# The third chunk's first head projections, written ahead of the last head's recurrence of the first two chunks

## The chip, the cores and the metric

One core of a Trainium2 chip runs the kernel. Its five engines each work off a queue of their own: TensorE (PE, with its weight loads as PEld), VectorE (DVE), ScalarE (ACT), GpSimd (POOL) and SyncE (SP), which here only issues transfers. The metric is the device time of one execution in microseconds; the figure for a kernel is the median of its runs.

## The reference, cut to what matters

One decoder layer over 1024 tokens of width 1024, all in 32-bit floats:

```python
h = _rmsnorm(x, norm_mix_w) * (1 + sc1) + sh1
q, f_logit, i, g, u = split(h @ w_in)          # four heads of 128, then S5's u
o_hg = _hgrn2(q, f_logit, i, g, lb)            # a gated linear recurrence over time, per head
o_s5 = _s5(u, ...)                             # a diagonal state space model, gelu, a gated unit
x = x + gt1 * (concat([o_hg, o_s5]) @ w_out)
h2 = _rmsnorm(x, norm_ffn_w) * (1 + sc2) + sh2
x = x + gt2 * _peer(h2, ...)                   # product keys, top 16 of 16384 experts, 8 heads
return _rmsnorm(x, final_norm_w)
```

For a head, `_hgrn2` makes a forget gate f, a key 1 - f, a query and a value from the projections, runs a state of 128 by 128 through time, normalizes each output row by its root mean square, and multiplies by a gate made of g.

## The kernel before, in words

The tokens are worked in four chunks of 256 (numbers 0 to 3). Activations stand transposed, features on the partitions, so every projection is a row of eight accumulating matmuls of a 128 by 128 weight tile with 256 columns; a 32-bit matmul shows as two records in the trace. `proj2` makes a pair of such products into one bank named `mm`, with weights that SP loads into four buffers named `w2`.

The program text begins with the conditioning and the norms, and then a loop of eight turns (line 1314), each with the scan of one batch of four S5 groups (`s5_scan`), the tables for the batch two turns on (`s5_tables`) and one piece of the heads of chunks 0 and 1, which are worked together (`head_pieces(0, True)`, line 1238). A piece is either `hgrn_in` of a head (line 669: four `proj2`, their sigmoids, the logarithm and running sum of f, and four transposes of the value at line 705) or `hgrn_out` of a head (line 710: the recurrence). By turns 0 to 7 the pieces are in 0, in 1, out 0, in 2, out 1, in 3, out 2, out 3. In turn 6 the norm of chunk 2 is written ahead of the piece.

`hgrn_out` has eight levels (line 742 is the matmul of seven of them, line 752 that of the eighth). Each level's operands come from DVE and an exponential on ACT, and its scores are copied by a mask into one tile `sc` that all heads share. Then follow the transposes at 765, the state update, the products with state and scores (781 and 782), the squares on ACT (787), their sum and the reciprocal root on DVE (789 to 246), the scaling (792) and transposes of the result (795), which go with the gate into a tile `mixr`.

Behind the loop stand `row_consts` (eight small transposes at line 1200, which copy a gate into a row and store it), the load of the keys, and then a list of steps in `ORDER` (line 60), worked by `step` (line 1277). In it `h2` is the next piece of chunk 2, whose pieces take two heads at once: in 0, in 2, out 0, out 2. `g0` is the gelu and gated unit of S5 for chunk 0, `o0` the output projection of chunk 0, which needs all four heads of chunk 0; `N0` is its second norm, `r0` and `s0` its scores, `p0` its choice of experts. After the list come the other stages: experts of 384 tokens by gathered rows, and those of 640 tokens by dense products.

The order on an engine is made before the launch. A planner simulates the program, and on every engine it lets the instruction that is earliest in the program text go first among those that its simulation finds ready. Each engine then works its queue strictly in that order, waiting where an operand is not there. Buffers of one name are given out in turn; the names here are `mm`, `tr` and `hg` (two banks each) and the working tiles of the heads (`f`, `k`, `b`, `q`, `gg`, `v`, `sf`, `xx`, `z`, mostly two).

Of the kernel before, what the change touches and what calls it, by code (L numbers as in the profile page):

```python
# [43 lines left out]
NGB = G // GB  # L44
# [12 lines left out]
PF = 0.2  # L57
PRB = 3
N2B = 6
ORDER = "h2 g0 o0 N0 r0 s0 s0 s0 s0 p0 h2 n3 g1 h2 h2 h3 o1 h3 N1 r1 s1 h3 s1 p1 g2 h3 X o2 Y g3 N2 s1 s1 o3 N3 R2 s2 s2 p2 s2 s2 s2 p3 s2 s2 s2 Z"  # L60
SLAB = 8
NROW = 5
NH = {}
# [26 lines left out]
def hymba_kernel(  # L90
# [96 lines left out]
    def ada(n0, n1, pool=None):  # L187
        for n in range(n0, n1):
            at = T(pool, [P, D], F32, "ada", bufs=10) if pool else T(gp, [P, D], F32, "row", bufs=NROW)
            nc.sync.dma_start(at, ada_t[n])  # L190
            nc.vector.tensor_tensor_reduce(
                out=at, in0=at, in1=cond["B"], scale=1.0, scalar=0.0, op0=ALU.mult, op1=ALU.add,
                accum_out=mod[:, n : n + 1],
            )
        TT(mod[:, n0:n1], mod[:, n0:n1], adab[:, n0:n1], ALU.add)
# [4 lines left out]
    def load_x(c, rows=False):  # L200
        t0, nt = CHUNKS[c]
        if rows:
            xt = [T(gp, [P, D], F32, "row", bufs=NROW) for _ in range(NBC)]
        else:
            xt = [T(tp, [P, D], F32, "xh", bufs=NBC) for _ in range(NBC)]
        for i, xi in enumerate(xt):
            nc.sync.dma_start(xi, x[t0 + i * P : t0 + (i + 1) * P, :])
        return xt
# [67 lines left out]
    def norm_T(xt, scol, bcol, t0=None, diags=None, ks=range(0, KD, 2)):  # L276

        diags = diags or diags_of(xt)
        ng = 0 if t0 is None else min(max(T0D - t0, 0), TC)
        res = []  # L280
        for k in ks:
            pt = T(ps, [P, 2, TC], F32, "tr", bufs=2)
            hf32 = pair(tp, F32, "hT", 8)
            for i in range(2):
                for tb in range(NBC):
                    nc.tensor.matmul(
                        pt[:, i, tb * P : (tb + 1) * P], xt[tb][:, (k + i) * P : (k + i + 1) * P], diags[tb], start=True, stop=True
                    )
                ACT(hf32[:, i], pt[:, i], AF.Identity, scale=scol[:, k + i : k + i + 1], bias=bcol[:, k + i : k + i + 1])
            res += both(hf32)  # L290
            if ng:

                pn = T(ps, [P, ng // P, 2, P], F32, "tr", bufs=2)
                for i in range(2):
                    for tb in range(ng // P):
                        nc.tensor.transpose(pn[:, tb, i, :], hf32[:, i, tb * P : (tb + 1) * P], ident)
                nn = pair(tp).rearrange("p a t -> p (a t)")[:, : 2 * ng].rearrange("p (b d) -> p b d", b=ng // P)
                nc.scalar.copy(nn, pn.rearrange("p b i d -> p b (i d)"))
                nc.scalar.dma_start(h2d[t0 : t0 + ng, k * P : (k + 2) * P].rearrange("(b p) d -> p b d", p=P), nn)
            if t0 is not None and ng < TC:  # L300

                nc.sync.dma_start(
                    h2s[k : k + 2, :, t0 + ng - T0D : t0 + TC - T0D].rearrange("k p t -> p k t"), hf32[:, :, ng:]
                )
        return res
# [286 lines left out]
    def s5_out(c):  # L592
        mixT = [None] * 4
        c0 = CHUNKS[c][0] // CT
        V3 = lambda t: t.rearrange("p (s c) -> p s c", s=CT)
        yts, ysp = [], []
        for m in range(0, 4, 2):
            yt = pair(tb_["p"], F32, "yt", 2)
            for i in range(2):
                nc.scalar.dma_start(  # L600
                    V3(yt[:, i]), ys[:, 4 * (m + i) : 4 * (m + i) + 4, :, c0 : c0 + TC // CT].rearrange("s h g c -> (h g) s c")
                )
            ACT(yt, yt, AF.Gelu)
            yts.append(yt)
            ysp += both(yt)
        for m in range(0, 4, 2):
            pt = proj2(w_glu, m, ysp, 4)
            sgm = pair(tp)
            for i in range(2):
                ACT(sgm[:, i], pt[:, i], AF.Sigmoid, bias=glub[:, m + i : m + i + 1])  # L610
            mx = pair(tb_["p"], F32, "mix", 2)
            for i in range(2):
                TT(mx[:, i].rearrange("p (c s) -> p s c", s=CT), V3(yts[m // 2][:, i]), V3(sgm[:, i]), ALU.mult)
            mixT[m : m + 2] = both(mx)
        return mixT
# [189 lines left out]
    def out_proj(c, mixT, xt):  # L805
        t0 = CHUNKS[c][0]
        for m in range(0, KD, 2):
            pt = proj2(w_out, m, mixT)
            mt = pair(tp)
            for i in range(2):  # L810
                ACT(mt[:, i], pt[:, i], AF.Copy, scale=mod[:, 16 + m + i : 17 + m + i])
            pn = T(ps, [P, NBC, 2, P], F32, "tr", bufs=2)
            for i in range(2):
                for tb in range(NBC):
                    nc.tensor.transpose(pn[:, tb, i, :], mt[:, i, tb * P : (tb + 1) * P], ident)
            for tb in range(NBC):
                xs = xt[tb][:, m * P : (m + 2) * P]
                TT(xs, xs, pn[:, tb].rearrange("p i d -> p (i d)"), ALU.add)
        for tb in range(NBC):
            r = t0 + tb * P  # L820
            nc.sync.dma_start(x1d[r : r + P, :], xt[tb])
# [416 lines left out]
    def head_pieces(c, two=False):  # L1238

        t = {}  # L1240
        outs = []
        far = T(gp, [P, 2, 2, TC], F32, "acc") if c == 2 else None

        def last(h):
            outs.append(hgrn_out(hp, c == NCK - 1, h, t.pop(h), two, None if far is None else far[:, h // 2]))
            if not two:
                raws.setdefault(c, []).append((outs[-1][:, 0], outs[-1][:, 1]))

        for h in range(0, HEADS, 1 if two else 2):
            if len(t) == 2:  # L1250
                last(min(t))
                yield
            t[h] = hgrn_in(hp, h, hTs[c], hTs[c + 1] if two else None)
            yield
        for h in sorted(t):
            last(h)
            yield
        if two:
            for i in range(2):
                raws[c + i] = [(outs[h][:, i], outs[h + 1][:, i]) for h in range(0, HEADS, 2)]  # L1260
# [16 lines left out]
    def step(what, c):  # L1277

        nonlocal rp
        if what == "n":  # L1280
            hTs[c] = norm_T(*pre[c][:1], s1c, mod[:, 0:8], None, pre[c][1])
            heads[c] = head_pieces(c)
        elif what == "h":
            next(heads[c])
        elif what == "g":
            mixes[c] = s5_out(c)
        elif what == "o":
            xts[c] = load_x(c, c == NCK - 1)
            hg = [r for two in raws[c] for r in two]
            out_proj(c, hg + mixes[c], xts[c])  # L1290
        elif what == "N":
            h2Ts[c] = norm_T(xts[c], s2c, mod[:, 24:32], CHUNKS[c][0])
        elif what in "rR":
            routes[c] = score(c, h2Ts[c], h2Ts[c + 1] if what == "R" else None)
            next(routes[c])
        elif what == "s":
            next(routes[c])
        elif what == "p":
            choose(rp, c)
        elif what == "X":  # L1300
            next(heads[NCK - 1], None)
            hpx.close()
        elif what == "Y":
            rpx.close()
            rp = tb_["r"] = rp2x.enter_context(tc.tile_pool(name="rp2", bufs=1, side="right"))
        elif what == "Z":
            tbx.close()

    hgrn_consts(hp)
    with tc.tile_pool(name="sp", bufs=1) as sp:  # L1310
        prm = s5_setup(sp)
        tabs = [s5_tables(sp, b, prm, "hg") for b in range(2)]
        pieces = head_pieces(0, True)
        for b in range(NGB):
            s5_scan(sp, b, tabs[b])
            if b + 2 < NGB:
                tabs.append(s5_tables(sp, b + 2, prm, "tr"))
            if b == N2B:
                step("n", 2)
            next(pieces, None)  # L1320
            if b < 4:
                ada(16 + 8 * b, 24 + 8 * b)
            if b == PRB:
                for c in (2, 3):
                    pre[c] = load_x(c, True)
                    pre[c] = pre[c], diags_of(pre[c])
        for _ in pieces:
            pass
# [6 lines left out]
    rp2x = ExitStack()  # L1335
    for w in ORDER.split():
        step(w[0], int(w[1:] or 0))
# [111 lines left out]
```

## Time and profile before

| what | value |
|---|---|
| median of 3 runs | 2981.1 us (2968.72 to 2986.83) |
| profiled execution | 2974.75 us, its span 2973.0 us |
| PE busy | 2782.4 us (94%) |
| PEld busy | 2492.3 us (84%) |
| DVE busy | 2464.2 us (83%) |
| ACT busy | 1093.4 us (37%) |
| mean granted TensorE clock | 0.976 |

Times inside the execution count from the start of its span. The loop of eight turns ends, and the list begins, at about 400 us; the dense stage starts near 1000 us. Busy time of PE counts overlapping records once. "Idle before" of a row is the time that its engine did nothing just ahead of it, with what ended the wait.

### The profile page before, as it was taken

The numbers are of one execution on the slowest core, as the hardware profiler recorded it, in microseconds if no ns is written. First come the engines' busy times: TensorE is split into PE (matmuls) and PEld (weight loads), VectorE is DVE, ScalarE is ACT, GpSimd is POOL, SyncE is SP. The second block draws the span as 40 slices with busy tenths as digits, with TensorE's granted clock in tenths as the row PEclk, the third lists the DMA queues.
The fourth block names the chain that finished last, engine by engine and source line by source line (L and its number), as shares of the span: only waits on it lengthen the run. The fifth ranks groups of instructions, "written<-read, shape, count | busy, mean of one in ns | idle before, by whom it ended". The sixth has DMA issues, their size and how long they took to land.

```text
span 2973.0 us, 46130 instructions
## 1 busy us (share of the span) xinstructions
PE 2782.4 (94%) x16071; PEld 2492.3 (84%) x16071; DVE 2464.2 (83%) x5598; ACT 1093.4 (37%) x2405; POOL 1143.7 (38%) x1043
## 2 busy tenths in 40 slices
PE   6899989989989799999999999999999999999995
PEld 5777978778878799989998888888888888888874
DVE  7869745977799999998568888978888888888988
ACT  3224431423310688979423322222222222222222
POOL 1765100231222002333344554545555556445552
PEclk9899989999999999999999999999999999999997
DMA  9822334686766358999999999989999899999986
GB/s 335 267 82 68 109 117 160 223 286 194 250 226 191 120 195 306 349 337 358 363 340 364 327 312 330 334 310 342 348 343 335 299 337 319 322 324 321 319 302 226
DMA packets 376265, 816.69 MB, mean 275 GB/s; under 512 B 60128, under 2 KB 153952, under 8 KB 370912
## 3 DMA queue, kind: packets, MB, share of 16 engines
q0 software_dynamic: 110592, 402.70, 38.4%
q1 hardware_dynamic: 227248, 388.74, 37.7%
q10 hardware_dynamic: 38192, 22.31, 2.7%
q8 instruction: 126, 2.06, 0.3%
q14 instruction: 107, 0.88, 0.1%
HBM read 732.27 MB, written 81.36 MB: 274 GB/s over the span
## 4 chain that ended last, share of the span: by engine, by line
PE 33%; DVE 19%; issue 19%; DMA 15%; POOL 10%; ACT 4%; POOLq 0%; ACTq 0%; DVEq 0%; SPq 0%
PE mm L1087 10%; PE mm L326 10%; POOL row L957 8%; DMA row<-in_v_rows_dram,ei 7%; PE hg L1163 3%; PE s L1163 3%; PE tr L1163 2%; DVE row L982 2%; DVE acc L998 2%; DMA row<-in_u_rows_dram,ei 2%; ACT oL L1047 2%; DMA vraw<-in_v_rows_dram 2%; DMA S<-sd 1%; DVE v L256 1%; PE hg L742 1%
## 5 line engine op out<-in xcount | busy, mean ns | idle before, releaser
L1087 PE MATMUL mm<-h2T,w 128*128 128x320 f32 x6144 | 943.5, 312 | 37.0 <-ACT S L1089 26.2
L1087 PEld LDWEIGHTS mm<-h2T,w 128*128 128x128 f32 x6144 | 913.9, 189 | 47.6 <-ACT S L1089 31.3
L957 POOL DMA_INDIRECT row<-in_u_rows_dram,ei x384 | 455.5, 1186 | 1148.9 <-DVE dots L982 648.1
L957 POOL DMA_INDIRECT row<-in_v_rows_dram,ei x384 | 523.2, 1363 | 486.5 <-DVE acc L998 400.4
L326 PE MATMUL mm<-hT,w 128*128 128x256 f32 x2304 | 529.4, 384 | 3.8 <-ACT tmp L610 2.6
L998 DVE SCALAR_TENSOR_TENSOR acc<-row,dots,acc 128x1024 f32<-128x1024 f32 x381 | 487.7, 1280 | 44.6 <-DMA row<-in_v_rows_dram,ei 41.3
L326 PEld LDWEIGHTS mm<-hT,w 128*128 128x128 f32 x2304 | 434.1, 193 | 61.5 <-ACT tmp L610 3.0
L982 DVE CUSTOM_DVE_ANT_0 row<-row,h2n 128x1024 f32<-128x1024 f32 x384 | 462.2, 1216 | 26.5 <-DMA row<-in_u_rows_dram,ei 25.7
L1163 PE MATMUL hg<-v,W 128*128 128x512 f32 x1296 | 352.5, 394 | 13.9 <-DVE v L256 5.5
L1163 PE MATMUL s<-v,W 128*128 128x512 f32 x1296 | 347.4, 391 | 2.2 <-DVE dacc L1176 1.1
L255 ACT CAST v<-vraw 128x512 fp32r<-128x512 f32 x256 | 158.5, 620 | 514.1 <-DMA vraw<-in_v_rows_dram 268.2
L1163 PE MATMUL tr<-v,W 128*128 128x512 f32 x1248 | 338.2, 392 | 8.4 <-DVE dacc L1176 4.2
L1163 PEld LDWEIGHTS hg<-v,W 128*128 128x128 f32 x1296 | 244.4, 190 | 69.5 <-DVE v L256 8.7
L1163 PEld LDWEIGHTS s<-v,W 128*128 128x128 f32 x1296 | 242.6, 188 | 55.4 <-DVE dacc L1176 2.8
L1163 PEld LDWEIGHTS tr<-v,W 128*128 128x128 f32 x1248 | 234.5, 189 | 59.7 <-DVE dacc L1176 5.5
L256 DVE TENSOR_TENSOR v<-vraw,v 128x512 fp32r<-128x512 f32 x256 | 175.4, 686 | 88.9 <-ACT v L255 87.0
L256 DVE TENSOR_TENSOR w<-raw,w 128x512 fp32r<-128x512 f32 x256 | 175.3, 686 | 70.5 <-ACT w L255 64.5
L255 ACT CAST w<-raw 128x512 fp32r<-128x512 f32 x256 | 158.2, 621 | 172.8 <-PE mm L1087 159.1
L1047 ACT ACTIVATE oL<-oA,self 128x128 f16<-128x128 f16 x640 | 196.3, 414 | 4.6 <-DVE self L1033 3.9
L1089 ACT ACTIVATE S<-mm 128x320 f32<-128x320 f32 x256 | 109.3, 439 | 206.3 <-PE mm L1087 165.2
L255 ACT CAST W<-S 128x640 fp32r<-128x640 f32 x128 | 93.1, 729 | 216.9 <-PE s L1163 65.1
L1106 DVE TENSOR_TENSOR S<-S,gt 128x640 f32<-128x640 f32 x128 | 104.1, 818 | 39.8 <-DMA S<-sd 37.6
(375 smaller groups left out, 3140.1 us busy)
## 6 DMA issues: line engine op xcount, KB each, us to landing
raw<-in_u_t_dram SPq DMA_DIRECT2D x256, 256.0 KB
vraw<-in_v_rows_dram SPq DMA_DIRECT2D x256, 256.0 KB
gd<-Gs SPq DMA_DIRECT2D x40, 1024.0 KB
gt<-gd SPq DMA_DIRECT2D x32, 1280.0 KB
w<-in_w_in_dram SPq DMA_DIRECT2D x56, 512.0 KB
w<-in_w_q_dram SPq DMA_DIRECT2D x48, 512.0 KB
sd<-S SPq DMA_DIRECT2D x64, 320.0 KB
S<-sd SPq DMA_DIRECT2D x64, 320.0 KB
```

Of the source, the lines that this page charges most:

```text
L255: nc.scalar.copy(hi, src)
L256: return nc.vector.tensor_tensor(lo, src, hi.bitcast(F32), ALU.subtract)
L326: ins = nc.tensor.matmul(out, w[:, k * P : (k + 1) * P], rhs[k], start=(k == 0), stop=(k == nk - 1))
L742: nc.tensor.matmul(pt[:, c * half : (c + 1) * half].rearrange("p (n l) -> p n l", l=lsz), blk(lh, c), two(blk(xx, c))[:, :, 1, :], start=T ...
L957: g = nc.gpsimd.indirect_dma_start(out=t, out_offset=None, in_=table, in_offset=bass.IndirectOffsetOnAxis(ap=idx, axis=0))
L982: nc.vector.tensor_tensor_reduce(out=ut, in0=ut, in1=h2, scale=1.0, scalar=0.0, op0=ALU.mult, op1=ALU.add, accum_out=dots[:, j : j + 1],)
L998: STT(acc, vt, w[:, j : j + 1], acc, ALU.mult, ALU.add)
L1047: nc.scalar.mul(Al[:, i], at(A, i), sL[:, t8 + i : t8 + i + 1])
L1087: nc.tensor.matmul(pt, wk[:, i, kc], h2T[k][:, j, cs_], start=(n == 0), stop=(n == 3 * KD - 1))
L1089: ACT(g[:, cs_], pt, AF.Gelu)
L1106: TT(gv, gv, gtile[0][:, :, e % IG, :], ALU.mult)
L1163: nc.tensor.matmul(pv[tb], ws[e][:, a, tb * P : (tb + 1) * P], v2[:, b, :], start=(e == s and n == 0), stop=(e == s + SLAB - 1 and n == 2),)
```

## The change

The first `h2` of the list, the projections of heads 0 and 1 of chunk 2, is taken from the list and written into the last turn of the loop, ahead of that turn's piece (the recurrence of head 3 of chunks 0 and 1). The same instructions are issued. In the program text they now stand ahead of that recurrence, of `row_consts` and of the load of the keys; before they stood behind all three.

```diff
-ORDER = "h2 g0 o0 N0 r0 s0 s0 s0 s0 p0 h2 n3 g1 ...
+ORDER = "g0 o0 N0 r0 s0 s0 s0 s0 p0 h2 n3 g1 ...
...
             if b == N2B:
                 step("n", 2)
+            if b == NGB - 1:
+                step("h", 2)
             next(pieces, None)
```

## Rows read from the trace of the kernel before

**Rows 1.** The page: span, then each engine's busy time, share and instructions.

```profile
span 2973.0 us, 46130 instructions
...
PE 2782.4 (94%) x16071; PEld 2492.3 (84%) x16071; DVE 2464.2 (83%) x5598; ACT 1093.4 (37%) x2405; POOL 1143.7 (38%) x1043
```

**Rows 2.** Windows: length, each engine's busy time (instructions), clock, DMA share, GB/s.

```profile
360.00:380.00 20.00, 20.00 (x123) 18.41 (x122) 10.79 (x27) 10.90 (x17) 0.00 (x0) 1.00 0.36 117
380.00:400.00 20.00, 10.34 (x56) 9.25 (x56) 11.33 (x37) 9.86 (x14) 0.00 (x0) 0.75 0.25 56
```

**Rows 3.** Timeline of PE, third head: start, length, line, operation, count [idle before].

```profile
314.89 1.00 PE L742 MATMUL hg<-xx,k 128*128 128x64 f32 x8
...
320.42 1.03 PE L326 MATMUL mm<-hT,w 128*128 128x256 f32 x4
...
340.22 0.39 PE L781 MATMUL hg<-st,xx 128*128 128x128 f32 x2
```

**Rows 4.** Timeline of PE, last head's recurrence and the hole behind it.

```profile
356.31 1.00 PE L742 MATMUL hg<-xx,k 128*128 128x64 f32 x8
357.16 4.96 PE L326 MATMUL mm<-hT,w 128*128 128x256 f32 x22
...
363.69 4.54 PE L326 MATMUL mm<-hT,w 128*128 128x256 f32 x20
...
369.79 4.54 PE L326 MATMUL mm<-yt,w 128*128 128x256 f32 x20
...
375.89 0.61 PE L765 MATMUL tr<-ident,z 128*128 128x128 f32 x4
...
382.37 1.53 PE L326 MATMUL mm<-mixr,w 128*128 128x256 f32 x6 [0.20 <-DMA w<-in_w_out_dram]
383.74 0.38 PE L781 MATMUL hg<-st,xx 128*128 128x128 f32 x2
...
385.30 0.39 PE L782 MATMUL hg<-v,sc 128*128 128x128 f32 x2
395.16 1.11 PE L795 MATMUL tr<-ident,xx 128*128 128x128 f32 x4 [9.47 <-DVE xx L792]
...
396.49 1.80 PE L742 MATMUL hg<-xx,k 128*128 128x64 f32 x8
```

**Rows 5.** Timeline of ACT: a table load, the late Gelus, the squares.

```profile
342.60 1.28 ACT L676 ACT_TABLE_LOAD   x1
343.89 0.60 ACT L676 ACTIVATE sf<-mm 128x512 f32<-128x512 f32 x1
...
358.37 1.28 ACT L603 ACT_TABLE_LOAD   x1 [5.00 <-DMA yt<-ys]
...
384.69 1.28 ACT L603 ACT_TABLE_LOAD   x1 [4.54 <-DMA yt<-ys]
...
390.41 0.58 ACT L787 ACTIVATE z<-hg 128x512 f32<-128x512 f32 x1
```

**Rows 6.** Timeline of DVE: the first level's operand; the sum of squares.

```profile
352.34 0.42 DVE L727 TENSOR_TENSOR xx<-f,q 128x256 f32<-128x256 f32 x1
...
391.02 0.69 DVE L789 TENSOR_REDUCE ms<-z 128x4 f32<-128x512 f32 x1 [5.96 <-ACT z L787]
```

**Rows 7.** Timeline of PE: the last of the eight row transposes, the value's.

```profile
413.46 0.38 PE L1200 MATMUL tr<-ident,diag 128*128 128x128 f32 x2
...
417.13 0.60 PE L705 MATMUL tr<-ident,sf 128*128 128x128 f32 x4
```

**Rows 8.** Timeline of SP's queue: the keys, the last weights of the projections.

```profile
349.64 0.33 SPq L1333 DMA_DIRECT2D keyst<-in_keys_dram  x1
351.32 0.33 SPq L321 DMA_DIRECT2D w<-in_w_in_dram  x1
```

**Rows 9.** Windows of the later stages, columns as in rows 2.

```profile
440.00:560.00 120.00, 115.47 (x603) 102.02 (x603) 79.67 (x482) 31.52 (x50) 3.27 (x3) 1.00 0.46 146
560.00:1000.00 440.00, 404.34 (x2113) 358.22 (x2112) 373.25 (x1472) 107.09 (x178) 102.01 (x98) 0.95 0.69 229
```

More of the change, by code (lines that the diff above doesn't have):

```diff
@@ L59 @@
 N2B = 6
-ORDER = "h2 g0 o0 N0 r0 s0 s0 s0 s0 p0 h2 n3 g1 h2 h2 h3 o1 h3 N1 r1 s1 h3 s1 p1 g2 h3 X o2 Y g3 N2 s1 s1 o3 N3 R2 s2 s2 p2 s2 s2 s2 p3 s2 s2 s2 Z"
+ORDER = "g0 o0 N0 r0 s0 s0 s0 s0 p0 h2 n3 g1 h2 h2 h3 o1 h3 N1 r1 s1 h3 s1 p1 g2 h3 X o2 Y g3 N2 s1 s1 o3 N3 R2 s2 s2 p2 s2 s2 s2 p3 s2 s2 s2 Z"
 SLAB = 8
```

## The prediction

> **What bounds the kernel now.** I read the page first: matmuls are busy 94% of the span, weight loads 84%, VectorE (DVE) 83% [rows 1]. No engine has slack over the whole, so time is won or lost where TensorE (PE) stands still. The windows of twenty microseconds around the change come next: PE is never idle from 360 to 380, and from 380 to 400 it is busy 10.34 us of 20 at a mean granted clock of 0.75 [rows 2]. That is the only large hole in the stretch that the change touches.
>
> The timeline of PE tells what is in it. The head projections that the change moves (the rows mm<-hT) begin at 320.42 as a filler below the third head's recurrence and the last S5 scan [rows 3]. The last head's recurrence has its first level on PE at 356.31; by then 86 of the 128 projection records are done. The other 42 follow in two bursts, of 22 and 20 records, between its levels; then come the records of the gated unit of S5 (32, yt, in two rows) and the first 12 of the output projection (mixr, rows of 2, 4 and 6), and at 385.69 the recurrence's last product is out [rows 4]. There PE stops for 9.47 us: the output projection has multiplied the three heads that exist and waits for the fourth, whose final transposes (L795) start at 395.16 [rows 4]. I call that instant the gate.
>
> The timeline of ACT tells why the hole is so long. The square of the recurrence's output (L787) could go at 385.69 but starts at 390.41: ahead of it in ACT's queue stands a Gelu of the second chunk, which sat 4.54 us until its load of ys landed [rows 5]. The squares, their sum, the reciprocal root and the scaling then take from 390.41 to the gate, 4.75 us [rows 4 to 6]. So 4.7 us of the hole is a queue accident and 4.8 us is the tail's own latency.
>
> **What the change does.** It adds and removes no instruction. In the written order 64 matmuls of 8 weight tiles (128 records), four ACT passes, their table loads, some seven DVE operations, four transposes (L705) and 8 weight loads on SP go from behind the last recurrence and the eight gate-row transposes (L1200) to ahead of them. The planner gives the earlier instruction first call on an engine. What was ahead already stays: 86 of 128 records, and the sigmoids, f, k and the scan that feed them.
>
> **Step 1, the 42 records.** They no longer yield to the recurrence. 22 records run from 357.16 to 361.96 or so: 4.96 us as merged, 20 take 4.54 [rows 4], thus near 0.22 us each, and 42 cost 9.2 us. The first level, whose operand DVE starts at 352.34 [rows 6], waits for PE until 356.31 + 9.2 = 365.5. Bounds: 0, if the planner finds a hole for the level between two projections, and +9.2.
>
> **Step 2, the recurrence without those bursts.** It took 27.4 us from its first level to its first product with the state (356.31 to 383.74) [rows 4]. The third head's took 25.3 us (314.89 to 340.22) [rows 3]. I take the shorter, because only 44 filler records (9.7 us) are left to stand in its way. The first product falls at 390.8, the last at 390.8 + 1.95 = 392.8. Bounds: PE has the same records to run up to there, and it ran them gapless to 385.69, so 385.7 is the earliest; 385.7 + 9.2 = 394.9 is the latest.
>
> **Step 3, the tail.** The load that the late Gelu waits for can go once the first chunk's gated unit has freed a buffer, and that unit's records follow the same projections on PE in either order [rows 4]; so I leave ACT free at about 390.4, as before. At 392.8 nothing is left of the 4.7 us. The gate comes at 392.8 + 4.75 = 397.6, that is 2.4 us later than 395.16. So the change loses about 7 us ahead of the accident and gets 4.7 of them back from it.
>
> **Step 4, the transposes L705.** The two banks named tr are given out in program order: L705 stands at 417.13, right behind the last of L1200, although its input was ready long before [rows 7]. Moved ahead of the recurrence's own tr tiles it runs in the recurrence's shadow, and 0.4 us of PE leaves the dense output projection. It takes a bank ahead of L765. That transposition ran at 375.89 and the last projection would end near 365.5, ten microseconds earlier, so nobody waits for it.
>
> **Step 5, SP and POOL.** The last of the 8 weight loads was issued at 351.32, behind the keys at 349.64 [rows 8], and used after 363: twelve microseconds of cover. The keys load is needed only when the scores begin, after the output projection; the store of the gate row comes after L1200. POOL has nothing in this stretch. Cost 0. If that cover were gone, PE would wait for one load.
>
> **Step 6, table loads of ACT.** Gathering the projections' Sigmoid and Ln ahead of the recurrence's Exp can save a table load or add one. A load takes 1.28 us, and the next ACTIVATE starts 1.29 us after it [rows 5]; ACT is busy 10.9 us of 20 there [rows 2]. I count 0, with 1.3 us either way inside the bounds above. The Trainium skill (ScalarE: Activation LUTs, What ACT_TABLE_LOAD costs) adds a drain of about 1380 ns to each load of 1283 ns; the load's length agrees, the drain is not seen between these two rows, and by the page one more switch would be worth an estimated 2.7 us.
>
> **The clock.** After the hole the same eight matmuls of a level take 1.80 us where they took 1.00 [rows 4], the lower of two levels (1.2 and 2.4 GHz). Of the work up to 400 that can have cost at most half of 4.8 us, 2.4. A closed hole gives it back; a longer one can cost as much again. I count 0.
>
> **Sum.** +2.4 - 0.4 = +2.0 us on the profiled execution's 2974.75 us (span 2973.0) [rows 1], thus 2976.8. That execution lies 6.35 us under the median of 2981.1, so the forecast is **2983 us**. About 1% (30 us) is what a measurement of this kernel can tell from no change.
>
> **Rivals.**
>
> *The gate moves by the whole 9.2 us.* The Gelu accident moves along with it, or the recurrence needs its 27.4 us again. For it: DVE's part is a chain that no PE filler sets. Against it: the 4.54 us are ended by a landing [rows 5]. With the clock's 2.4: +11.6, **2993 us**. It decides from the point when the recurrence's last product comes after 393.
>
> *The hole closes.* The planner interleaves so that the last product stays at 385.7 and places the Gelu behind the square: -4.7 - 2.4 - 0.4 = -7.5, **2974 us**. For it: PE had its records gapless before. Against it: work that is not urgent goes ahead of work that is.
>
> *Nothing happens.* The planner ran two thirds of the projections ahead of the recurrence anyhow [rows 3, 4], and the rest may come out in the same order: **2981 us**.
>
> *The whole later plan shifts, to the worse.* The list order after 440 is made anew from shifted instants, and accidents like the Gelu fall elsewhere. PE idles 4.5 us of 440 to 560 and 35.7 of 560 to 1000 [rows 9]; where heads, scores and the first gathers share that stretch, a second 35.7 us would give **3019 us**. It decides if a third chunk's recurrence comes late against its output projection. The same *to the better* would have to take away three quarters of those 40 us: 2951 or less.
>
> **Numbers.** The forecast 0.45; whole delay 0.18; hole closed 0.12; nothing 0.15; a worse later plan 0.06; a better one 0.04. Within 1% are the first four: 0.90; slower 0.06; faster 0.04. The range takes in 2974 and 2993 and, on either side, the spread of the runs of before (2968.7 to 2986.8, 12.4 under the median and 5.7 over) with a few microseconds of a shifted later plan: 2960 to 3005. It leaves out the two ends of the later plan.
>
> **What would show it.** Right: L705 ahead of L765; one row of some 40 projection records before the first L742 of the last head, which stands near 365; L795 between 395 and 400; the Gelu's wait over before L787 is ready. Wrong, step 1: the first level still near 356 with projections behind it. Step 2: a recurrence longer than 27.4 us or well under 25. Step 3: L787 again held by a landing. The whole argument is wrong if the windows from 440 to 1000 hold a difference larger than that of 300 to 440.

## The result and the profile after

The changed kernel takes 3000.04 us (median of 6 runs, 2996.69 to 3007.00), the kernel before, measured beside it, 2979.45: a ratio of 1.0076, 95% interval 1.0058 to 1.0094. That is some 0.8% slower: inside the range, 17 us above the forecast of 2983, and by the prediction's bound of 1% still no change. But the interval is clear of 1, so the change does slow the kernel, by ten times the 2 us that the prediction summed up.

The page after answers to [rows 1]. The same 16071 records keep PE busy 14.1 us longer; the span grew by 25.2, so 11.1 us are new idle time and the rest is slower records. These are two single executions: that of before lies 4.7 us under its median, and the medians are 20.6 us apart. The 29 instructions that the page counts more are semaphore operations, which the new order brings: e3 below, with the old text, has 46159 too. Their number does not make the time, for e8 has only 46126 and is slower still.

```profile
span 2998.2 us, 46159 instructions
...
PE 2796.5 (93%) x16071; PEld 2508.3 (84%) x16071; DVE 2464.4 (82%) x5598; ACT 1093.5 (36%) x2405; POOL 1122.4 (37%) x1043
```

The windows of after, columns as in [rows 2], the stretches of [rows 2, 9] first:

```profile
360.00:380.00 20.00, 20.00 (x112) 18.04 (x111) 10.09 (x27) 10.80 (x15) 0.00 (x0) 1.00 0.48 134
380.00:400.00 20.00, 12.62 (x84) 11.53 (x84) 13.50 (x40) 11.12 (x16) 0.00 (x0) 0.92 0.28 59
440.00:560.00 120.00, 116.58 (x587) 103.13 (x588) 78.69 (x481) 28.79 (x46) 0.12 (x1) 0.95 0.45 141
560.00:1000.00 440.00, 407.97 (x2135) 361.47 (x2133) 369.15 (x1465) 106.66 (x175) 103.28 (x101) 0.95 0.69 230
1000.00:1600.00 600.00, 565.56 (x4490) 551.50 (x4490) 512.32 (x1240) 423.94 (x1266) 172.78 (x144) 0.97 0.83 302
...
2940.00:3020.00 80.00, 29.23 (x116) 23.34 (x116) 48.19 (x90) 14.44 (x32) 14.59 (x12) 0.81 0.45 156
```

The last two stretches in the kernel before:

```profile
1000.00:1600.00 600.00, 575.82 (x4591) 561.47 (x4590) 516.79 (x1240) 426.39 (x1270) 177.95 (x148) 0.99 0.86 310
...
2940.00:3020.00 80.00, 5.56 (x25) 4.28 (x23) 26.89 (x62) 7.82 (x17) 5.21 (x5) 0.84 0.20 72
```

Where the change was made nothing is lost: 380 to 400 has 9.7 us of idle PE before and 7.4 after, at a better clock. The dense stage is another matter. From 1000 to 1600 PE is idle 34.4 us where it was idle 24.2, with 101 records fewer done, and at 2940 the changed kernel has 116 records left where before had 25. Lined up by the same instruction, after stands 6.8 us behind before at the first upward product (L1087, near 994), 15.5 at the first downward one (L1163, 1577), 23.5 near 1966 and 29.1 near 2868. The first of these says little: e4 below, which has the queues of after, reaches that product at 996.8, and e1 and e2, which have before's order up to it from 520 us on, at 995.0 and 998.8.

The timeline of PE, answering to [rows 3, 4, 7]:

```profile
317.77 1.00 PE L742 MATMUL hg<-xx,k 128*128 128x64 f32 x8
...
359.19 9.23 PE L326 MATMUL mm<-hT,w 128*128 128x256 f32 x42
368.26 1.00 PE L742 MATMUL hg<-xx,k 128*128 128x64 f32 x8
...
372.21 0.60 PE L705 MATMUL tr<-ident,sf 128*128 128x128 f32 x4
...
384.97 0.60 PE L765 MATMUL tr<-ident,z 128*128 128x128 f32 x4
...
389.70 0.39 PE L781 MATMUL hg<-st,xx 128*128 128x128 f32 x2
...
391.52 0.39 PE L782 MATMUL hg<-v,sc 128*128 128x128 f32 x2
396.77 1.12 PE L795 MATMUL tr<-ident,xx 128*128 128x128 f32 x4 [4.86 <-DVE xx L792]
```

At the third head's first level this execution is 2.88 us behind that of before (317.77 against 314.89), though PE's queue up to there is the same; so 2.88 is taken off each time here. The first level of the last head then comes at 365.4 and the gate (L795) at 393.9: 1.3 us *earlier* than the 395.16 of before, with a hole of 4.86 us where there were 9.47. The runs below bear it out: from the third head's first level to the gate it is 79.0 to 79.9 us in the three kernels with the whole change (after, e2, e4) and 80.0 to 81.1 in before, e11 and the six pinned kernels with the old text.

The timeline of ACT, answering to [rows 5]:

```profile
386.26 1.28 ACT L603 ACT_TABLE_LOAD   x1 [1.88 <-DVE xx L738]
387.55 0.63 ACT L603 ACTIVATE yt<-yt 128x512 f32<-128x512 f32 x1
...
391.44 0.63 ACT L756 ACTIVATE e<-b 128x512 f32<-128x512 f32 x1 [0.95 <-DVE sth L778]
392.01 0.60 ACT L787 ACTIVATE z<-hg 128x512 f32<-128x512 f32 x1
```

The late Gelu no longer waits for its landing, and the square follows the last product at once.

So where are the 25 us? One wait of PE in the dense stage (1600 to 2940) stands out: total, times, longest. First after, then before:

```profile
PE mm L1087 <- ACT S L1089: 29.7, 10, 4.3
```

```profile
PE mm L1087 <- ACT S L1089: 13.6, 8, 2.6
```

This wait grew by 16.1 us, but PE's whole idle time there only from 36.6 to 42.2, as other waits got shorter. The windows, after and then before:

```profile
1600.00:2300.00 700.00, 685.89 (x3586) 606.59 (x3586) 590.36 (x830) 197.18 (x350) 345.46 (x271) 1.00 0.95 329
2300.00:2940.00 640.00, 611.95 (x3089) 534.95 (x3088) 543.09 (x632) 159.34 (x282) 321.88 (x242) 0.98 0.90 316
```

```profile
1600.00:2300.00 700.00, 690.99 (x3618) 610.89 (x3617) 598.14 (x837) 195.94 (x349) 358.73 (x274) 1.00 0.95 333
2300.00:2940.00 640.00, 612.41 (x3046) 528.33 (x3045) 544.77 (x636) 161.24 (x287) 331.57 (x241) 0.98 0.90 315
```

So the wait marks the mechanism and is not the whole sum. In e1 and e3 below, which differ in nothing but the later order, the same idle time goes from 32.6 to 48.7.

An upward product (24 records) needs one of two banks `mm`, and a bank comes free when ACT has taken half a gate out of it by a Gelu (L1089). One such wait, in the timelines of ACT and PE after:

```profile
2371.23 0.61 ACT L255 CAST v<-vraw 128x512 fp32r<-128x512 f32 x1
2384.08 0.62 ACT L255 CAST v<-vraw 128x512 fp32r<-128x512 f32 x1 [12.24 <-DMA vraw<-in_v_rows_dram]
2384.60 0.43 ACT L1089 ACTIVATE S<-mm 128x320 f32<-128x320 f32 x1
```

```profile
2371.52 1.18 PE L1087 MATMUL mm<-h2T,w 128*128 128x320 f32 x7
...
2374.84 6.17 PE L1087 MATMUL mm<-h2T,w 128*128 128x320 f32 x41
2385.09 6.04 PE L1087 MATMUL mm<-h2T,w 128*128 128x320 f32 x24 [4.08 <-ACT S L1089]
```

The same place before, again ACT and then PE:

```profile
2348.56 0.61 ACT L255 CAST v<-vraw 128x512 fp32r<-128x512 f32 x1
2354.86 0.44 ACT L1089 ACTIVATE S<-mm 128x320 f32<-128x320 f32 x1 [5.69 <-PE mm L1087]
2362.55 0.62 ACT L255 CAST v<-vraw 128x512 fp32r<-128x512 f32 x1 [7.25 <-DMA vraw<-in_v_rows_dram]
```

```profile
2352.03 9.84 PE L1087 MATMUL mm<-h2T,w 128*128 128x320 f32 x66
...
2364.70 12.35 PE L1087 MATMUL mm<-h2T,w 128*128 128x320 f32 x72 [2.60 <-ACT S L1089]
```

Before, ACT's queue holds the Gelu first and then the cast of a v that is still on its way; the Gelu goes as soon as its product is out, and PE gets a third product done ahead of its stop. After, the two stand the other way round. The product is complete near 2377.4 (7 records, and 17 more at 0.15 us from 2374.84), but its Gelu sits until 2384.60 behind a cast that waited 12.24 us for its landing; PE fills the second bank and stops after 48 records. It is the accident of [rows 5], a ready Gelu behind an instruction with a late load, made many times. The Trainium skill (PSUM — Partial Sum Buffer, Engine vs sequencer instructions) calls ACT's queue strictly first in, first out; these rows agree, the ready Gelu not having passed the cast. In all 9 waits of this kind over 0.5 us after, the instruction just ahead of the Gelu on ACT is a cast of v that itself stood 7 to 12 us; before, in 3 of 8. In the other 5 of before such a cast, with 5 to 7 us of standing, is three places ahead of the Gelu, as at 2362.55 above: before's order shortens the accident and does not remove it.

The changed text touches none of these instructions. But the order of every queue is made from the whole program, and it came out anew: side by side, the lists of the queues from about 520 us on (those of e1 and e3 below) hold another instruction in 4340 of 12437 places on PE, 2214 of 3496 on DVE, 1116 of 2102 on ACT, 191 of 841 on SP and none of 768 on POOL. On PE, DVE and ACT over nine tenths of these lie behind 1000.

### The profile page after: what moved, and what is told of

It is laid out like the page before. It is cut to its first block, busy times and chain, and to the rows that moved or that the text cites. A ratio compares the mean times of both kernels' runs of the same rounds, so it can differ in the third digit from the quotient of the medians.

```text
span 2998.2 us, 46159 instructions
## 1 busy us (share of the span) xinstructions
PE 2796.5 (93%) x16071; PEld 2508.3 (84%) x16071; DVE 2464.4 (82%) x5598; ACT 1093.5 (36%) x2405; POOL 1122.4 (37%) x1043
## 4 chain that ended last, share of the span: by engine, by line
PE 47%; DVE 15%; DMA 14%; issue 13%; POOL 7%; ACT 3%; ACTq 0%; DVEq 0%; POOLq 0%; SPq 0%
PE mm L1087 16%; PE mm L326 14%; POOL row L957 5%; DMA vraw<-in_v_rows_dram 4%; PE hg L1163 4%; PE s L1163 4%; DMA row<-in_v_rows_dram,ei 3%; PE tr L1163 3%; DMA row<-in_u_rows_dram,ei 3%; DVE row L982 2%; DVE acc L998 2%; ACT oL L1047 1%; DMA S<-sd 1%; PE s L1051 1%; PE s L1052 1%
## 5 line engine op out<-in xcount | busy, mean ns | idle before, releaser
L1087 PE MATMUL mm<-h2T,w 128*128 128x320 f32 x6144 | 955.1, 315 | 51.3 <-ACT S L1089 42.0
L1087 PEld LDWEIGHTS mm<-h2T,w 128*128 128x128 f32 x6144 | 924.2, 191 | 62.2 <-ACT S L1089 46.9
L957 POOL DMA_INDIRECT row<-in_v_rows_dram,ei x384 | 503.6, 1312 | 518.5 <-DVE acc L998 417.1
L1163 PE MATMUL hg<-v,W 128*128 128x512 f32 x1296 | 352.2, 394 | 15.8 <-DVE v L256 7.2
L1163 PE MATMUL s<-v,W 128*128 128x512 f32 x1296 | 346.8, 391 | 1.6 <-DVE v L256 1.5
L1163 PE MATMUL tr<-v,W 128*128 128x512 f32 x1248 | 336.8, 391 | 4.5 <-DVE v L256 2.4
L1163 PEld LDWEIGHTS hg<-v,W 128*128 128x128 f32 x1296 | 244.0, 190 | 70.2 <-DVE v L256 10.3
L1163 PEld LDWEIGHTS s<-v,W 128*128 128x128 f32 x1296 | 243.4, 189 | 53.3 <-DVE v L256 2.3
L1163 PEld LDWEIGHTS tr<-v,W 128*128 128x128 f32 x1248 | 234.0, 188 | 54.3 <-DVE v L256 3.7
L1089 ACT ACTIVATE S<-mm 128x320 f32<-128x320 f32 x256 | 109.7, 441 | 204.6 <-PE mm L1087 182.1
```

Source lines behind the costliest of these rows:

```text
L957: g = nc.gpsimd.indirect_dma_start(out=t, out_offset=None, in_=table, in_offset=bass.IndirectOffsetOnAxis(ap=idx, axis=0))
L1087: nc.tensor.matmul(pt, wk[:, i, kc], h2T[k][:, j, cs_], start=(n == 0), stop=(n == 3 * KD - 1))
L1089: ACT(g[:, cs_], pt, AF.Gelu)
L1163: nc.tensor.matmul(pv[tb], ws[e][:, a, tb * P : (tb + 1) * P], v2[:, b, :], start=(e == s and n == 0), stop=(e == s + SLAB - 1 and n == 2),)
```

## The experiments

Theory A: the loss is the re-made order of the later queues. Theory B: it is the moved projections themselves (their place, and what it does to the work after them). Eight kernels fix each queue's order from about 520 us on, by an edge from each instruction to the next one on its engine that demands order and no wait (shortened):

```diff
     ...
+    pin(nc, tc)
+def pin(nc, tc):
+    ...
+        for x, y in zip(queue, queue[1:]):
+            tc.add_manual_dep(ins[y], ins[x].name, NoSync, reason="pin")
```

Everything that is computed stays. "Wait" in this table is that of PE's L1087 for ACT's S, from 1600 to 2940, in us. The medians of before beside them are 2978.21 (e1 to e4), 2977.79 (e5 to e8) and 2979.97 (e9 to e12). The ratio is not the quotient of the medians; the two differ by up to 0.0016 (e6).

| kernel | text and order up to 520 us | order behind | median, us | ratio to before | wait |
|---|---|---|---|---|---|
| e1 | before | before | 2976.85 | 1.0003 (0.9990 to 1.0016) | 11.7 |
| e2 | changed | before | 2979.04 | 1.0008 (0.9992 to 1.0024) | 13.2 |
| e3 | before | changed | 2999.52 | 1.0080 (1.0060 to 1.0100) | 32.9 |
| e4 | changed | changed | 3000.94 | 1.0086 (1.0065 to 1.0107) | 26.9 |
| e5 | before | changed from 520 to 1370 only | 2986.70 | 1.0023 (1.0006 to 1.0040) | 17.4 |
| e6 | before | changed from 1370 on | 3005.07 | 1.0076 (1.0046 to 1.0106) | 29.4 |
| e9 | before | changed from 1370 to 1585 only | 2984.45 | 1.0015 (0.9997 to 1.0034) | 12.3 |
| e10 | before | changed from 1585 on | 2995.43 | 1.0044 (1.0023 to 1.0065) | 29.3 |
| e7 | projections behind `o0` | its own | 3004.57 | 1.0080 (1.0049 to 1.0112) | 27.1 |
| e8 | projections behind `g0` | its own | 3014.20 | 1.0114 (1.0086 to 1.0142) | 28.4 |
| e11 | projections behind the last recurrence | its own, the same as before's | 2980.53 | 1.0009 (0.9993 to 1.0026) | 11.4 |
| e12 | projections in turn 6 | its own | 3017.84 | 1.0124 (1.0091 to 1.0157) | 31.4 |

**e1 to e4, text against later order.** The edit is the function above, with one or the other list of the later order.

> The kernel before, with the order of every engine's queue from about 520 us on written down and pinned to what the planner itself made of the kernel before (no instruction differs; edges of issue order only). All theories: the same as before, 2979 us, ratio 1.000 within 0.3%. If it is not, pinning itself costs time and the other three runs are read against this one.

> The changed kernel (projections ahead of the last recurrence, so the local order up to 430 us is that of the change), with every queue from 520 us on pinned to the order of the kernel before. Theory A, the planner's later order costs the time: about 2978 to 2982 us, ratio 0.999 to 1.002, since in the two traces the gate at L795 lies 1.3 us earlier against the step before it. Theory B, the moved projections themselves cost it, in a way that the gate doesn't show: about 3000 us, ratio 1.007.

> The kernel before, with its own text and its own order up to 430 us, and every queue from 520 us on pinned to the order that the planner made of the changed kernel. Theory A: about 3000 us, ratio 1.006 to 1.009. Theory B: about 2979 us, ratio 1.000. If it lies between, both parts matter.

> The changed kernel with its own later order pinned. All theories: as the changed kernel, about 3000 us, ratio 1.007.

e1 and e4 show that the pins cost nothing that these runs can tell: both give the kernel that they copy. e2 has the whole change up to 520 us and is no slower than before; e3 has nothing of the change but the later order, and has the whole loss. The wait goes with the order. In e2, and then in e3:

```profile
PE mm L1087 <- ACT S L1089: 13.2, 8, 3.5
```

```profile
PE mm L1087 <- ACT S L1089: 32.9, 10, 5.7
```

Theory B has fallen: the moved projections are worth 1.0008, with an interval that takes in 1.

**e5, e6, e9, e10, which part of the later order.** The text is that of before, and a part of the list is exchanged, cut where both orders have issued the same instructions.

> The kernel before, pinned as in the runs above, with the order of the changed kernel only from 520 us to about 1370 us (scores, choice of experts, most of the gate maps and of the early upward products) and its own order behind that. Theory A1, the later order loses in several places and the losses add: in the traces the pinned later order had lost some 7 us against the other by then, so about 2985 us, ratio 1.002 to 1.003. Theory A2, only the dense stage loses, and what is late before it is made up: ratio 1.000.

> The kernel before, pinned, with its own order to about 1370 us and the order of the changed kernel behind it (the last early products and the dense stage). Theory A1: the other 12 to 15 us, about 2992 us, ratio 1.004 to 1.006. Theory A2: all of it, about 3000 us, ratio 1.007 to 1.009.

> The text of before with every queue pinned from about 520 us on: before's order, but from about 1370 to about 1585 us (the last early products of the dense stage, up to the first products with v) the order of the changed kernel, and behind that before's order again. Theory A (the loss is made of many small waits, wherever the re-made order lies): lining up e6 with e1 by the dense products gives 7 to 12 us by the end of this stretch, so a ratio of 1.0025 to 1.004, 2985 to 2990 us. Rival A2 (the loss is all in the reordered dense turns behind): 1.000, 2978 us. Rival A3 (a late first v sets everything back once, and the rest only follows): 1.007, 2999 us.

> The text of before with every queue pinned: before's order up to about 1585 us, the order of the changed kernel behind (the dense turns). Theory A: e6 against e1 lost some 29 of its 41 us of dense stage behind 1583 us, less what e6 spreads: a ratio of 1.004 to 1.007, 2990 to 2999 us, with waits of PE for ACT's S of 2 to 5 us at the places where e6 has them. Rival A2 (all of it here): 1.0076, 3001 us. Rival A3 (a late first v sets everything back): 1.000, 2978 us.

The three pieces e5, e9 and e10 add to 0.82%, the loss of e3. Over half of it (0.44%) is behind 1585 us, where ACT's list differs from before's in 108 places, each by at most five, as the Gelu and the cast above; e10 has the long wait there, e9 has not:

```profile
PE mm L1087 <- ACT S L1089: 29.3, 9, 5.9
```

```profile
PE mm L1087 <- ACT S L1089: 12.3, 8, 4.4
```

So the loss does not sit in one place. The new order ahead of 1370 us (e5) and that behind 1585 (e10) each cost time, with intervals clear of 1; e9's takes in 1 as well as the value that theory A expected. The late first v (A3) falls, for e9's interval ends at 1.0034 and A3 said 1.007. That the dense turns alone make it (A2) falls by e5; e10 speaks against it more weakly, its interval ending at 1.0065, below A2's 1.0076 but not below the lower end of e3's. e6 came out larger than theory A1 expected, at the value of its A2; its interval reaches both.

What makes e5's 0.23% was not separated: one wait of L1051 for the gates (Gs, L1054) ahead of 1600 is 3.8 us in e5 and 1.6 in e1, and in the dense stage, where e5 has before's order, the wait for S is 17.4 where e1 has 11.7. Nor did any run exchange the order of one engine alone. In e10 the list of DVE differs in 1352 places and that of PE in 1223, so it is shown that the order costs the time, while that ACT's casts are what costs it there is argued from the waits.

**e7, e8, e11, e12, other places for the same projections.** Nothing is pinned, and the planner makes each order. In e7 and e8 the step stays in the list and only goes later:

```diff
-ORDER = "h2 g0 o0 N0 r0 ...
+ORDER = "g0 o0 h2 N0 r0 ...      (e7)
+ORDER = "g0 h2 o0 N0 r0 ...      (e8)
```

> Nothing pinned. The moved projections go the other way: behind the output projection of chunk 0 in the list of steps, later than in the kernel before, so no recurrence waits for them. In the planned queues the order of ACT and of SP in the later stages comes out as that of the changed kernel, and that of PE and DVE nearly so. Theory A (the later order costs): about 3000 us, ratio 1.005 to 1.010, though nothing was moved ahead. Theory B (the projections ahead of the recurrence cost): 2979 us or less, ratio 1.000 or below.

> Nothing pinned. The projections stand behind the gated unit of chunk 0, one step later than in the kernel before. The planner makes a third later order of it, unlike both. Theory A: the time is that of its later order, anywhere from 0.5% faster to 1% slower, and not tied to the move. Theory B: as the kernel before, ratio 1.000.

In e11 and e12 it is taken from the list as in the change and written elsewhere in the loop:

```diff
             next(pieces, None)
+            if b == NGB - 1:
+                step("h", 2)          # e11
...
             if b == N2B:
                 step("n", 2)
+                step("h", 2)          # e12
```

> Nothing pinned. The step h2 is taken from the list and written into the last turn as in the change, but behind that turn's recurrence instead of ahead of it, so it only passes the row transposes and the keys' load. The order that it gives behind 520 us is that of before, instruction by instruction. Theory A (the time follows the later order): ratio 1.000, 2978 us, the same within 0.2%. Rival B (writing the projections earlier costs by itself): between 1.000 and 1.008, about 1.004.

> Nothing pinned. The step h2 is written one piece earlier still, in turn 6, right behind the norm of chunk 2, ahead of the recurrences of heads 2 and 3. Its later order is a fourth one, different from before's in some 4500 places of PE's queue. Theory A (a re-made later order is worth some tenths of a per cent either way and is not told by how far the projections move): 0.996 to 1.012, with the difference behind 520 us. Rival B (the time grows with how early the projections stand): above the change's 1.008, with the difference ahead of 520 us.

e11 moves the projections past the row transposes and the keys' load but not past the recurrence; the later order comes out as before's (its trace has the same instructions in the same places on PE, DVE and ACT behind 1000 us) and so does the time. e7 moves them the other way, later, and loses as much as the change does, with an order that behind 1000 us is the changed kernel's on the same three engines. e8, also later but with an order of its own, lost 1.14%, a little more than the 1% that its expectation allowed, though its interval reaches that. So the loss doesn't follow how early the projections stand. e12 is the one with a loss of its own at the place of the edit: PE waits for a Gelu and the gate comes 12.5 us later than the 395.16 of before.

```profile
373.42 2.08 PE L326 MATMUL mm<-yt,w 128*128 128x256 f32 x4 [6.38 <-ACT yt L603]
...
407.61 1.12 PE L795 MATMUL tr<-ident,xx 128*128 128x128 f32 x4 [4.85 <-DVE xx L792]
```

Its expectation, all of the difference behind 520 us, missed that; but of 43.3 us of span some 31 still come later, with the same wait (31.4 us). Every new order that the planner made is slower than before's, by 0.8 to 1.2% (e12's own loss near 400 us included), and no version beat before. That before's order is a lucky one among many fits this, but four orders don't show it.

## Why the prediction came out as it did

The forecast was "no change beyond 1%", and its local argument held up; the loss came from a place that its sum had priced at nothing. That the time still lies inside the range is luck: the range was widened for the spread of the runs and "a few microseconds of a shifted later plan", and the later plan cost some 20.

- **Step 1 was right.** 42 records in one row, first level at 365.4 against 365.5.
- **Step 2 was mis-sized.** From first level to first product with the state the recurrence took 21.4 us (368.26 to 389.70), not 25.3: the third head's run, taken as a measure, had 112 records of other work between its products (314.89 to 340.22), the last head's after only 48. That these slowed it is argued. The last product is out at 389.0, not 392.8. The prediction had named a recurrence "well under 25" as the sign against this step.
- **Step 3 was right in kind.** The Gelu's accident was absorbed and the tail took 4.86 us (4.75 expected); with step 2's size the gate comes 1.3 us earlier, not 2.4 later. The sign of the local effect was wrong by less than a run can tell: e2 gives 1.0008.
- **Step 4 was right.** L705 runs at 372.21, ahead of L765 at 384.97, and neither waits.
- **Step 5 was right.** PE runs without a gap from 358.76 to 368.26, so no weight was late.
- **Step 6 was right.** Both kernels make 74 table loads. The load at 386.26 takes 1.28 us and its ACTIVATE starts 1.29 after the load's start, so here too the drain that the Trainium skill (ScalarE: Activation LUTs, What ACT_TABLE_LOAD costs) adds is not seen.
- **The clock** gave back a little: 0.92 granted in 380 to 400, where it was 0.75.
- **The step that failed is the sum's silence about everything behind 440 us.** It is the rival "the whole later plan shifts, to the worse", held at 0.06. Its mechanism was the right one: the list order made anew, and accidents like the late Gelu falling elsewhere. Its place and price were not. It looked for a third chunk's recurrence between 560 and 1000 us and priced a doubling of 35.7 us; that stretch's idle time fell to 32.0. The loss stands behind it, in the dense stage, which [rows 9] stopped short of, and it is 20.6 us between the medians (25 between the profiled executions), not 36. The prediction's own last sentence named the first sign: a larger difference behind 440 than ahead of it. It only ended its window at 1000, where the sign can't be read: from the gate to the first upward product it is 604.1 us after and 599.0 before, but 598.8 in e4, which copies after, and 601.9 in e2.

A row of before shows where the risk lay: the 13.6 us that PE waits for S in eight places of the dense stage, where a Gelu stands close behind a cast of late data on ACT.

Open is what in the planner carries a shift near 400 us to queues behind 1000; its working was not traced. That it orders a cast ahead of a ready Gelu because it expects the load earlier than it lands is argued, not shown.

## What to carry to other kernels

Where a planner makes the order of all queues from one program, an edit has two effects: the local one, and a new draw of every later order. Look for the price of the second in the places of the whole trace where a ready instruction stands behind one that waits for a load on an in-order queue, not only in the stages next to the edit; no run here tests how well such a price foretells the time. To tell the two apart, pin the later order of the old kernel under the new text, and the new order under the old text: here these two runs showed that the edit is worth 1.0008 and the new draw 1.0080.

## What the runs showed of the hardware

A stop of PE can cost more than its length. Windows of after, ahead of and from the stop shown above:

```profile
2373.00:2383.00 10.00, 8.01 (x50) 7.40 (x48) 6.32 (x9) 0.00 (x0) 2.80 (x3) 1.00 1.05 384
2383.00:2393.00 10.00, 7.91 (x37) 7.78 (x38) 7.78 (x9) 3.37 (x7) 2.62 (x3) 0.66 0.61 200
```

A shorter stop before, in the timeline of PE and in the window behind it:

```profile
1940.64 10.82 PE L1087 MATMUL mm<-h2T,w 128*128 128x320 f32 x72 [0.58 <-ACT S L1089]
```

```profile
1940.00:1950.00 10.00, 9.42 (x65) 9.36 (x65) 10.00 (x13) 3.25 (x8) 4.68 (x4) 1.00 0.69 213
```

A stop of 3.42 us, in after again, and the window around it:

```profile
2135.77 3.79 PE L1087 MATMUL mm<-h2T,w 128*128 128x320 f32 x24 [3.42 <-ACT S L1089]
```

```profile
2134.00:2144.00 10.00, 8.23 (x45) 7.46 (x46) 8.59 (x14) 4.62 (x9) 4.10 (x3) 1.00 0.73 236
```

Behind the stop of 4.08 us the granted clock is 0.66 over ten microseconds (0.50 from 2385 to 2388, the lower of the two levels, and 1.00 again from 2391 to 2394), and the 24 records that follow take 6.04 us, 252 ns each, where the 41 ahead of it took 150: 2.4 us more, on top of the 4.08. Behind the stop of 0.58 us it stays at 1.00, and so it does behind that of 3.42 us, where the 24 records take 158 ns each. So not every stop of some microseconds is followed by a slow stretch; what decides it was not tested. The slow stretches are part of the 14.1 us by which PE's busy time grew with the same records; how large a part was not summed. Some 3 of the 14.1 had grown by the third head's recurrence, ahead of the change.
